# A decoder layer on one core: joint pairs of the FFN prepared one pair ahead, bank-freeing additions put in front, and token sums moved from GpSimd to VectorE

## The chip, the cores and the metric

The kernel runs on one core of a Trainium2 chip. The metric is the device time of one execution in microseconds; several runs are timed and their median is taken. One further execution is profiled. TensorE does the matrix products, VectorE and ScalarE the elementwise work, GpSimd some elementwise work and DMA issues, and SyncE (SP) issues most DMAs.

## What is computed

One layer: RWKV-7 time mixing and indexer-selected sparse attention side by side, merged by gates, then a dense FFN. The change lies in the FFN, d_model 1024, 1024 tokens, FFN width 2816 (22 tiles of 128):

```python
merged = g_a * (y_a @ w_o_rwkv) + g_b * (y_b @ w_o_att)
h = h + merged @ w_out
z = rmsnorm(h, norm2_g) @ w_ffn_in
z_gate, z_up = jnp.split(z, 2, axis=-1)
h = h + (jax.nn.silu(z_gate) * z_up) @ w_ffn_out
return rmsnorm(h, normf_g)
```

## The kernel before

Everything is held with channels on the partitions, in two halves of 512 tokens. A product in float32 precision is made of three float32r matmuls: weights and activations are split into a high and a low part (`split`, L116 the high part on ScalarE, L117 the low part on VectorE), and hi*hi, hi*lo and lo*hi are added up in one PSUM bank (`mm3`, L146, L147, L151). A raw weight tile is loaded into a buffer `wst` (three of them in all), its parts go to `whi` and `wlo` (two of each). Three banks carry the name `acc`, five the name `mix`; a bank is free when VectorE has read it.

The order of TensorE is the order in which the program is written. The other engines are ordered by a scheduler that goes by priority and by its own estimate of time; what stands in `tc.high_priority()` (also called `urgent`) goes ahead. Once built, every engine and every DMA queue works strictly in its order, so an instruction that waits holds up all behind it.

The FFN is done in two ways. The first 8 tiles (`EARLY`) are ordinary: for each half `ffn_in` makes gate and up products of a tile and `ffn_out` adds the product with `w_fo` to h, which lives in DRAM (`d_h`), one output tile d of 8 at a time: load h (L1360), add the bank (L1361), store (L1362). For half 0 this runs as filler work beside RWKV and attention. The filler also holds `ahead(j)`, and half 1's attention loop calls `scaled` eight times: GpSimd adds zhi and zlo, multiplies by the row of norms and stores the normalized half 0 in `d_z`.

Tiles 8 to 21 are *joint*, both halves at once. Halves of the tokens, halves of the input channels and gate/up make a 2x2 by 2x2 block product, done with seven block products instead of eight (Winograd's form of Strassen's scheme). Two of the seven, on half 0 alone, are made by `ahead` and kept in `d_p`. The other five need sums of weight blocks and of token blocks:

- `combined` builds the token blocks t1, t2, t4 from half 1 (`h`) and half 0 (`d_z`, into two tiles `t`), with four GpSimd subtractions for each of four k (L1443), and splits them.
- `joint_in` handles one pair of gate and up tiles j: it loads both weights, makes four GpSimd sums (L1443, scratch tile `s1`, of which there is one), splits them to wb (in whi/wlo), wc (wchi/wclo) and wd (wdhi/wdlo, one buffer each for wc and wd), and then does five products of 12 matmuls: pa, pb, pc, pd, and a second one added into pc's bank (L1495 to L1499). Between them VectorE adds the banks: L1503 (pa), L1505 (pb), L1507 (pc), L1509 (pd), L1512 (pc again). The second product into pc's bank may not begin before L1507 has read it.

After each group of pairs (`JOINT`: 4, 3, 3 and 4 pairs) comes `ffn_out` for both halves, or `finish_out` after the last. A group boundary is the end of `ffn_out` and the start of the next group's first pair. The h tiles of `ffn_out` go through a ring of eight (`more`).

Of the kernel before, what the change touches and what calls it, by code (L numbers as in the profile page):

```python
# [11 lines left out]
F32 = mybir.dt.float32  # L12
# [14 lines left out]
EARLY = [(0, 8)]  # L27
# [23 lines left out]
def block_kernel(ctx: ExitStack, tc: tile.TileContext, ins: dict, outT: bass.AP, stop=None, dbg=None):  # L51
# [1131 lines left out]
    def merge(half, zp, zs, jp=None):  # L1183
# [59 lines left out]
        for d in range(8):  # L1243
# [8 lines left out]
            SY.dma_start(d_h[half][d], h[:, d, :])  # L1252
            sq.add(d, last=half == 1 and d == 7)
# [33 lines left out]
    def ffn_in(half, f, zs, g0, gn):  # L1287

        z, sq = zs[:2]
        for j in range(gn):  # L1290
            pg, pu = acc(), acc()
            src = [ins["w_ffn_in"][2 * (g0 + j) + i] for i in range(2)]
            if g0 + j == 0:
                ws = [weights(x) for x in src]
                first_ = mm3_late([pg, pu], ws, z)
                for i, n in enumerate(first_):
                    yield n
                    if i == 3 and half == 0:
                        sq.columns()
                if half == 0:  # L1300
                    zs.append(sq.row(bufs=2))
                    yield 4
            else:
                yield from mm3(pg, weights(src[0]), z)
                yield from mm3(pu, weights(src[1]), z)
            if half:
                swiglu(f, j, pg, pu)
                continue
            row, x, t = zs[2], tmp(), tmp()
            V.tensor_tensor(x, pg, row, op=ALU.mult)  # L1310
            silu(t, x)
            V.scalar_tensor_tensor(x, pu, 0.5, row, op0=ALU.mult, op1=ALU.mult)
            V.tensor_tensor(t, t, x, op=ALU.mult)
            split(f[0][:, j, :], f[1][:, j, :], t)
# [13 lines left out]
    def ahead(j, zs):  # L1328

        (zhi, zlo), _, row = zs  # L1330
        w = weights(ins["w_ffn_in"][2 * j])
        pss = [acc(), acc()]
        for i, ps in enumerate(pss):
            yield from mm3(ps, w, (zhi, zlo), nk=4, wk=4 * i, ak=4 * i)
# [8 lines left out]
    def scaled(k, zs):  # L1343

        (zhi, zlo), _, row = zs
        x = tmp()
        G.tensor_tensor(x, f32(zhi[:, k, :]), f32(zlo[:, k, :]), op=ALU.add)
        G.tensor_tensor(x, x, row, op=ALU.mult)
        SY.dma_start(d_z[k], x)

    def ffn_out(f, g0, gn, halves, ring=None):

        act = {h: tuple(x[:, gn * i:gn * i + gn, :] for x in f) for i, h in enumerate(halves)}

        def w(d):
            return weights(ins["w_fo"][d][:, g0:g0 + gn, :], gn)

        def add(d, half, ps):
            t = tmp() if ring is None else ring[:, (2 * d + half) % 8, :]
            SY.dma_start(t, d_h[half][d])  # L1360
            V.tensor_tensor(t, t, ps, op=ALU.add)  # L1361
            SY.dma_start(d_h[half][d], t)  # L1362

        first_ = [(d, half) for d in range(2) for half in halves][:2]
        ws = {d: w(d) for d in sorted({d for d, _ in first_})}
        pss = {x: acc() for x in first_}
        yield from mm3_last(list(pss.values()), [ws[d] for d, _ in first_], [act[h] for _, h in first_], gn)
        for d in range(8):
            for half in halves:
                ps = pss.get((d, half))  # L1370
                if ps is None:
                    if d not in ws:
                        ws[d] = w(d)
                    ps = acc()
                    yield from mm3(ps, ws[d], act[half], nk=gn)
                add(d, half, ps)
# [53 lines left out]
    def early(half, zp, zs):  # L1430

        for g0, gn in EARLY:
            f = act_tiles(zp, "f", ("s2", "s0"))
# [280 lines left out]
```

## Time and profile before

| | |
|---|---|
| median of 3 runs | 1774.36 us (1769.57 to 1774.5) |
| profiled execution, its own time | 1764.16 us |
| its span, first to last instruction | 1762.4 us |
| TensorE busy | 1690.7 us, 96% of the span |
| VectorE / ScalarE / GpSimd busy | 1175.9 / 824.5 / 233.5 us |
| mean granted TensorE clock | 0.990 |

Rows of a timeline show the start, the duration, the engine and line, the operation with output and inputs, its shape and, in brackets, how long the engine was idle before and what ended that. In the list of waits each row has the total, the number and the longest. Matmuls are pipelined: one of 512 columns is shown with 0.39 us, though the next begins 0.23 us after it.

### The profile page before, as it was taken

To read this page: it belongs to the slowest core of one execution; us is meant where nothing else is said; L and a number is where in the kernel's file an instruction comes from. 1 tells how busy PE (TensorE), PEld (TensorE's weight loads), DVE (VectorE), ACT (ScalarE), POOL (GpSimd) and SP (SyncE) were. 2 spreads that over 40 slices of the span, in tenths; PEclk is the share of its full clock that TensorE was granted. 3 is DMA by queue.
4 is the path that set the end of the run, shared out by engine and by line. 5 is a ranking of instruction groups with operands and counts; after the bars stand their busy time and mean duration, and the time that the engine had idled before them with its cause. 6 is when DMAs were issued, how large, how long until landed. Compare 5 with 4: busy or idle time off the path is not lost.

```text
span 1762.4 us, 26864 instructions
## 1 busy us (share of the span) xinstructions
PE 1690.7 (96%) x9952; PEld 1386.7 (79%) x9952; DVE 1175.9 (67%) x2253; ACT 824.5 (47%) x1585; POOL 233.5 (13%) x211
## 2 busy tenths in 40 slices
PE   8999999999999999999999899999899999999897
PEld 6888888788877777877887788778688877777787
DVE  5789899866576467857867555665744654655576
ACT  6365998454444787555334367333432221222231
POOL 0000000010022101001000351000600402130420
PEclk9999999999999999999999999999999999999999
DMA  5542224535375425653343883674336436465532
GB/s 208 162 144 95 99 96 142 162 101 178 104 206 158 132 99 177 203 145 117 104 119 124 253 221 121 221 245 149 116 108 195 132 128 215 135 203 163 202 109 96
DMA packets 149091, 268.14 MB, mean 152 GB/s; under 512 B 38704, under 2 KB 63984, under 8 KB 148832
## 3 DMA queue, kind: packets, MB, share of 16 engines
q1 hardware_dynamic: 125600, 192.59, 34.3%
q10 hardware_dynamic: 15552, 47.75, 8.6%
q0 software_dynamic: 7808, 26.09, 5.6%
q8 instruction: 78, 1.28, 0.3%
q14 instruction: 53, 0.43, 0.1%
HBM read 195.54 MB, written 70.83 MB: 151 GB/s over the span
## 4 chain that ended last, share of the span: by engine, by line
PE 67%; DVE 12%; ACT 7%; DMA 6%; issue 4%; POOL 4%; SPq 0%; POOLq 0%; DVEq 0%; ACTq 0%
PE acc L146 14%; PE acc L147 14%; PE acc L151 14%; PE acc L161 3%; PE mix L1495 2%; PE mix L1499 2%; PE mix L1497 2%; DVE wlo L117 2%; PE mix L934 2%; DMA wst<-in_w_ffn_in 2%; PE mix L1093 2%; ACT junk L984 2%; ACT junkl L984 1%; PE mix L1069 1%; POOL wst L1443 1%
## 5 line engine op out<-in xcount | busy, mean ns | idle before, releaser
L117 DVE TENSOR_TENSOR wlo<-wst,whi 128x1024 fp32r<-128x1024 f32 (+2 forms) x201 | 224.2, 1117 | 179.4 <-ACT whi L116 80.4
L116 ACT ACTIVATE whi<-wst 128x1024 fp32r<-128x1024 f32 (+2 forms) x201 | 186.9, 932 | 266.6 <-PE acc L147 194.0
L146 PE MATMUL acc<-zhi,whi 128*128 128x512 f32 x336 | 134.5, 400 | 8.9 <-ACT whi L116 5.6
L146 PE MATMUL acc<-u1hi,whi 128*128 128x512 f32 x352 | 140.7, 400 | 0.1
L147 PE MATMUL acc<-u1lo,whi 128*128 128x512 f32 x352 | 138.4, 393 | 0.0
L146 PE MATMUL acc<-u0hi,whi 128*128 128x512 f32 (+1 forms) x352 | 135.3, 387 | 1.7 <-DVE tmp L352 1.7
L147 PE MATMUL acc<-u0lo,whi 128*128 128x512 f32 (+1 forms) x352 | 133.8, 383 | 0.0
L147 PE MATMUL acc<-zlo,whi 128*128 128x512 f32 x336 | 132.6, 395 | 0.0
L146 PE MATMUL acc<-fhi,whi 128*128 128x512 f32 x236 | 92.9, 394 | 3.2 <-DVE more L1361 2.2
L147 PE MATMUL acc<-flo,whi 128*128 128x512 f32 x236 | 91.9, 389 | 0.0
L151 PE MATMUL acc<-u1hi,wlo 128*128 128x512 f32 x352 | 90.5, 396 | 0.0
L151 PE MATMUL acc<-zhi,wlo 128*128 128x512 f32 x336 | 87.4, 395 | 0.0
L151 PE MATMUL acc<-u0hi,wlo 128*128 128x512 f32 (+1 forms) x352 | 86.6, 385 | 0.0
L146 PEld LDWEIGHTS acc<-zhi,whi 128*128 128x128 f32 x336 | 64.0, 190 | 24.5 <-ACT whi L116 6.7
L146 PEld LDWEIGHTS acc<-u1hi,whi 128*128 128x128 f32 x352 | 67.4, 192 | 14.9 <-DVE tmp L343 0.5
L146 PEld LDWEIGHTS acc<-u0hi,whi 128*128 128x128 f32 x352 | 66.2, 188 | 15.1 <-ACT stg L116 2.1
L147 PEld LDWEIGHTS acc<-u1lo,whi 128*128 128x128 f32 x352 | 67.1, 191 | 13.3
L151 PEld LDWEIGHTS acc<-u1hi,wlo 128*128 128x128 f32 x352 | 65.7, 189 | 14.4 <-issue 1.2
L147 PEld LDWEIGHTS acc<-u0lo,whi 128*128 128x128 f32 x352 | 66.2, 188 | 12.2
L151 PEld LDWEIGHTS acc<-u0hi,wlo 128*128 128x128 f32 x352 | 64.0, 188 | 13.1 <-issue 0.7
L147 PEld LDWEIGHTS acc<-zlo,whi 128*128 128x128 f32 x336 | 64.0, 191 | 12.6
L151 PEld LDWEIGHTS acc<-zhi,wlo 128*128 128x128 f32 x336 | 62.9, 190 | 13.2 <-issue 0.3
(420 smaller groups left out, 3981.2 us busy)
## 6 DMA issues: line engine op xcount, KB each, us to landing
wst<-in_w_ffn_in SPq DMA_DIRECT2D x58, 512.0 KB, 4.0
wst<-in_w_in ACTq DMA_DIRECT2D x36, 512.0 KB, 3.9
wst<-in_w_in SPq DMA_DIRECT2D x27, 512.0 KB, 4.0
k<-d_k POOLq DMA_DIRECT2D x24, 512.0 KB, 8.5
more<-d_h SPq DMA_DIRECT2D x48, 256.0 KB, 3.6
d_h<-more SPq DMA_DIRECT2D x48, 256.0 KB, 3.8
h<-in_xT SPq DMA_DIRECT2D x32, 256.0 KB, 5.0
d_g<-tmp ACTq DMA_DIRECT2D x32, 256.0 KB, 3.0
```

Of the source, the lines that this page charges most:

```text
L116: A.activation(hi, x, AF.Copy)
L117: V.tensor_tensor(lo, x, hi.bitcast(F32), op=ALU.subtract)
L146: T.matmul(ps, whi[:, wk + k, :], ahi[:, ak + k, tok], start=k == 0, stop=False)
L147: T.matmul(ps, whi[:, wk + k, :], alo[:, ak + k, tok], start=False, stop=False)
L151: T.matmul(ps, wlo[:, wk + k, :], ahi[:, ak + k, tok], start=False, stop=k == nk - 1)
L161: T.matmul(ps, w[:, k, :], a[:, k, tok], start=k == 0 and w is whi and a is ahi, stop=k == nk - 1 and a is alo)
L934: T.matmul(ps[:, :w], iq[:, h, :], ik[:, i, c:c + w], start=i == 0, stop=i == 1)
L984: A.activation(junka[:, :n], y, AF.Sign, bias=z[:, i:i + 1], accum_out=cnt[:, i:i + 1])
L1093: T.matmul(py[64 * e:64 * e + 64, bi * 128:(bi + 1) * 128], v[:, j, 64 * e:64 * e + 64], pts[e][j // 4][:, j % 4, :], start=j == b, stop=j ...
L1495: T.matmul(ps, w[0][:, o + k, :], bhi[:, k, :], start=first_ and k == 0, stop=False, skip_group_check=not first_)
L1497: T.matmul(ps, w[0][:, o + k, :], blo[:, k, :], start=False, stop=False, skip_group_check=not first_)
L1499: T.matmul(ps, w[1][:, o + k, :], bhi[:, k, :], start=False, stop=k == 3, skip_group_check=not first_)
```

## The change

1. The weights of a joint pair are handled in two functions. `sums(j)` loads them and makes the four GpSimd sums, `blocks(j)` does the splits. Both are called for pair j+1 at the start of pair j; for the first pair of a group `sums` is called in the last pair of the group before, and `blocks` where `ffn_out` takes its last weight (d = 7). Pair 8 is prepared at d = 7 of half 1's early `ffn_out`.
2. In joint groups the raw output weights go to the two `t` tiles of `combined` instead of `wst`, and half 1 comes before half 0.
3. The additions of pa, pb and pc (now L1527, L1530, L1533) stand in `urgent()`.
4. `scaled` is gone. `merge(0)` stores the raw h in `d_z` as well; `combined` multiplies it by the norm's weight and the row on VectorE when it loads it, and its 16 subtractions are on VectorE too. It takes one of eight steps behind each early tile of half 1.

```diff
             SY.dma_start(d_h[half][d], h[:, d, :])
+            if half == 0:
+                SY.dma_start(d_z[d], h[:, d, :])
...
-    def scaled(k, zs):
-
-        (zhi, zlo), _, row = zs
-        x = tmp()
-        G.tensor_tensor(x, f32(zhi[:, k, :]), f32(zlo[:, k, :]), op=ALU.add)
-        G.tensor_tensor(x, x, row, op=ALU.mult)
-        SY.dma_start(d_z[k], x)
-
-    def ffn_out(f, g0, gn, halves, ring=None):
+    def ffn_out(f, g0, gn, halves, ring=None, raw=None, last=None):
...
         def w(d):
-            return weights(ins["w_fo"][d][:, g0:g0 + gn, :], gn)
+            if d not in ws:
+                src, st = ins["w_fo"][d][:, g0:g0 + gn, :], None
+                if raw is not None:
+                    with tc.high_priority():
+                        st = raw.tile([128, gn, 128], F32, tag="t", name="t", bufs=2)
+                        wq[0].dma_start(st, src)
+                ws[d] = weights(src, gn, st=st)
+                if d == 7 and last is not None:
+                    last()
+            return ws[d]
...
+        def part(ds):
+            for d in ds:
+                for half in reversed(halves):
+                    ps = pss.get((d, half))
+                    if ps is None:
+                        wt, ps = w(d), acc()
+                        yield from mm3(ps, wt, act[half], nk=gn)
+                    add(d, half, ps)
+
+        def open_():
+            for d in range(2):
+                w(d)
+                pss[d, halves[-1]] = acc()
+            yield from mm3_last(list(pss.values()), [ws[0], ws[1]], [act[halves[-1]]] * 2, gn)
+            yield from part(range(2))
...
+        def less(o, a, b):
+            V.tensor_tensor(o, a, b, op=ALU.subtract)
+
         for k in range(4):
...
-            SY.dma_start(a, d_z[k])
-            SY.dma_start(b, d_z[k + 4])
-            pool(ALU.subtract, a, lo, a)
+            for x, i in ((a, k), (b, k + 4)):
+                SY.dma_start(x, d_z[i])
+                V.scalar_tensor_tensor(x, x, par[:, P_N2 + i:P_N2 + i + 1], row, op0=ALU.mult, op1=ALU.mult)
+            less(a, lo, a)
             put(t1, k, a)
-            pool(ALU.subtract, lo, up, lo)
-            pool(ALU.subtract, up, up, a)
+            yield
+            less(lo, up, lo)
+            less(up, up, a)
             put(t2, k, up)
-            pool(ALU.subtract, b, b, up)
+            less(b, b, up)
             put(t4, k, b)
             yield
...
+    prepared = {}
+
+    def sums(j, jp):
+
         with tc.high_priority():
             g, u = (raw_weights(ins["w_ffn_in"][2 * j + e]) for e in range(2))
...
+    def joint_in(f, gn, i, j, bs, ring, jp):
+
+        wb, wc, wd = prepared.pop(j)
+        p1, t0, w, c = (ring[:, j % 2, e, :] for e in range(4))
+        SY.dma_start(ring[:, j % 2, 0:2, :], d_p[j])
+        if j + 1 < NFF:
+            sums(j + 1, jp)
+            if i + 1 < gn:
+                blocks(j + 1, jp)
...
         mm(pa, wb, 0, "t2")
-        V.tensor_tensor(p1, p1, pa, op=ALU.add)
+        with urgent():
+            V.tensor_tensor(p1, p1, pa, op=ALU.add)
...
-                run(ffn_out(f, g0, gn, [0, 1], more))
+                run(*ffn_out(f, g0, gn, [0, 1], more, jp, lambda: blocks(g0 + gn, jp)))
```

TensorE's instructions stand in the same order as before but for the half that comes first in an output tile. What moves is on the other engines. Below, the order of instructions at three places, before and then after.

VectorE at the boundary between the second and the third group, before: wlo, wclo and wdlo are splits of the next pair's weights, s is GpSimd's scratch sum, more the additions that free the output banks, ring the additions of a pair.

```order
L117 TENSOR_TENSOR wlo<-wst,whi 128x384
L1361 TENSOR_TENSOR more<-more,acc 128x512 x2
L117 TENSOR_TENSOR wclo<-wst,wchi 128x1024
L117 TENSOR_TENSOR wdlo<-wst,wdhi 128x512
L117 TENSOR_TENSOR wlo<-wst,whi 128x512
L117 TENSOR_TENSOR wlo<-s_14279,whi 128x512
L1361 TENSOR_TENSOR more<-more,acc 128x512 x3
L117 TENSOR_TENSOR wlo<-s_14381,whi 128x512
L117 TENSOR_TENSOR wlo<-wst,whi 128x512
L1503 TENSOR_TENSOR ring<-ring,acc 128x512
```

The same place after the change, where an output weight comes from t:

```order
L117 TENSOR_TENSOR wlo<-t,whi 128x384
L1362 TENSOR_TENSOR more<-more,acc 128x512 x2
L117 TENSOR_TENSOR wlo<-wst,whi 128x512
L117 TENSOR_TENSOR wlo<-s_13920,whi 128x512
L1362 TENSOR_TENSOR more<-more,acc 128x512 x2
L117 TENSOR_TENSOR wlo<-wst,whi 128x512
L117 TENSOR_TENSOR wlo<-s_14280,whi 128x512
L1362 TENSOR_TENSOR more<-more,acc 128x512
L1527 TENSOR_TENSOR ring<-ring,acc 128x512
```

The wclo and wdlo of the first pair are gone from here (they stand in the last pair of the group before), and one of the three last additions stands behind the second pair's splits.

VectorE in the second pair of the first group, before; the two wlo are the next pair's:

```order
L1512 TENSOR_TENSOR ring<-ring,mix 128x512
L117 TENSOR_TENSOR wlo<-s_13205,whi 128x512
L117 TENSOR_TENSOR wlo<-wst,whi 128x512
L1513 SCALAR_TENSOR_TENSOR ring<-ring 128x512
L1503 TENSOR_TENSOR ring<-ring,acc 128x512
L117 TENSOR_TENSOR flo<-ring,fhi 128x512
L1505 TENSOR_TENSOR ring<-ring,mix 128x512
L1507 TENSOR_TENSOR ring<-ring,mix 128x512
```

And after:

```order
L1538 TENSOR_TENSOR ring<-ring,mix 128x512
L1527 TENSOR_TENSOR ring<-ring,acc 128x512
L117 TENSOR_TENSOR wlo<-wst,whi 128x512
L117 TENSOR_TENSOR wlo<-s_13104,whi 128x512
L1539 SCALAR_TENSOR_TENSOR ring<-ring 128x512
L1530 TENSOR_TENSOR ring<-ring,mix 128x512
L117 TENSOR_TENSOR flo<-ring,fhi 128x512
L1533 TENSOR_TENSOR ring<-ring,mix 128x512
```

The first addition now stands ahead of both splits; the two splits have changed places.

ScalarE at the first early tile of half 1, before; t are high parts of the token blocks, zhi those of half 1, whi a weight:

```order
L1262 ACTIVATE zhi<-h 128x512 x3
L116 ACTIVATE t_12179<-t 128x512
L1262 ACTIVATE zhi<-h 128x512 x2
L1318 ACTIVATE tmp<-tmp 128x512
L116 ACTIVATE t_12180<-h 128x512
L116 ACTIVATE t_12181<-t 128x512
L116 ACTIVATE whi<-wst 128x1024
L1318 ACTIVATE tmp<-acc 128x512
```

And after:

```order
L1264 ACTIVATE zhi<-h 128x512 x5
L1317 ACTIVATE tmp<-tmp 128x512
L116 ACTIVATE whi<-wst 128x1024
L1317 ACTIVATE tmp<-acc 128x512
L116 ACTIVATE t_12139<-t 128x512
L116 ACTIVATE whi<-wst 128x1024
```

The token blocks' copies have moved behind the first weight copy of the second tile.

More of the change, by code (lines that the diff above doesn't have):

```diff
@@ L1285, in mm3_late, with ffn_in @@
             yield 8
[L1287 to L1314, printed above, removed]
+    def ffn_in(half, f, zs, j):
+        z = zs[0]
+        pg, pu = acc(), acc()
+        src = [ins["w_ffn_in"][2 * j + i] for i in range(2)]
+        if j == 0:
+            for i, n in enumerate(mm3_late([pg, pu], [weights(x) for x in src], z)):
+                yield n
+                if i == 3 and half == 0:
+                    zs[1].columns()
+            if half == 0:
+                zs.append(zs[1].row(bufs=2))
+                yield 4
+        else:
+            yield from mm3(pg, weights(src[0]), z)
+            yield from mm3(pu, weights(src[1]), z)
+        if half:
+            swiglu(f, j, pg, pu)
+            return
+        row, x, t = zs[2], tmp(), tmp()
+        V.tensor_tensor(x, pg, row, op=ALU.mult)
+        silu(t, x)
+        V.scalar_tensor_tensor(x, pu, 0.5, row, op0=ALU.mult, op1=ALU.mult)
+        V.tensor_tensor(t, t, x, op=ALU.mult)
+        split(f[0][:, j, :], f[1][:, j, :], t)
     def silu(t, x):
@@ L1333, in ahead @@
         for i, ps in enumerate(pss):
-            yield from mm3(ps, w, (zhi, zlo), nk=4, wk=4 * i, ak=4 * i)
+            yield from mm3(ps, w, zs[0], nk=4, wk=4 * i, ak=4 * i)
+        row = zs[2]
         p, x, t = tmp(), tmp(), tmp()
@@ L1362, in add @@
             SY.dma_start(d_h[half][d], t)
[L1364 to L1376, printed above, removed]
+        def part(ds):
[12 more added lines that the diff above has]
+            yield from part(range(2))
+        return [open_(), *(part([d]) for d in range(2, 8))]
     def norm_out(half, sq):
@@ L1428, in finish_out, with early @@
         run(before)
[L1430 to L1437 removed]
+    def early(half, zp, zs, last=None):
+        f = act_tiles(zp, "f", ("s2", "s0"))
+        return [ffn_in(half, f, zs, j) for j in range(EARLY)], ffn_out(f, 0, EARLY, [half], last=last)
     def f32(x):
@@ L1486, in joint_in, with blocks @@
             pool(ALU.subtract, g2, g2, g1)
-            split(wb[0][:, 0:4], wb[1][:, 0:4], g1)
+        prepared[j] = g, u, s1
+    def blocks(j, jp):
+        g, u, s1 = prepared[j]
+        with tc.high_priority():
+            wb = [wp.tile([128, 8, 128], F32R, tag=t, name=t) for t in ("whi", "wlo")]
+            wc = [jp.tile([128, 8, 128], F32R, tag=t, name=t) for t in ("wchi", "wclo")]
+            wd = [jp.tile([128, 4, 128], F32R, tag=t, name=t) for t in ("wdhi", "wdlo")]
+            split(wb[0][:, 0:4], wb[1][:, 0:4], g[:, 0:4])
             split(wb[0][:, 4:8], wb[1][:, 4:8], s1)
             split(wc[0], wc[1], u)
-            split(wd[0], wd[1], g2)
+            split(wd[0], wd[1], g[:, 4:8])
+        prepared[j] = wb, wc, wd
+    def joint_in(f, gn, i, j, bs, ring, jp):
[6 more added lines that the diff above has]
+                blocks(j + 1, jp)
         def mm(ps, w, o, b, first_=True):
@@ L1617, in block_kernel, with begin @@
         both = [zp0, zp1]
-        build = combined(both, *z1, jp)
-        bs = None
-        for i, n in enumerate(early(1, zp0, z1)):
-            if i % 12 == 11 and i < 48:
-                next(build)
-            if n == 0:
-                bs = next(build)
+        build = combined(both, z0[2], *z1, jp)
+        def begin():
+            sums(JOINT[0][0], jp)
+            blocks(JOINT[0][0], jp)
+        tiles_, outs = early(1, zp0, z1, begin)
+        for i, g in enumerate(tiles_):
+            run(g)
+            next(build)
+        bs = next(build)
+        run(*outs)
         more = jp.tile([128, 8, HT], F32, tag="t3", name="more")
```

36 lines of the change are left out of this document (16 added, 20 removed).

## The prediction

> **What bounds the kernel now.** The page of the profile comes first: TensorE is busy in 96% of the span, so whatever is to be won is the rest of it.
>
> ```profile
> span 1762.4 us, 26864 instructions
> PE 1690.7 (96%) x9952; PEld 1386.7 (79%) x9952; DVE 1175.9 (67%) x2253; ACT 824.5 (47%) x1585; POOL 233.5 (13%) x211
> ```
>
> Next, the busy time by stage (columns: stretch, length, then busy time of TensorE, its weight loads, VectorE, ScalarE, GpSimd). The stretches are the first early tiles of half 1, the other early tiles, and the middle groups of joint pairs.
>
> ```profile
> 1230.00:1282.00 52.00, 44.57 (x182) 34.62 (x181) 42.22 (x50) 23.04 (x35) 31.10 (x16) 0.97 0.37 108
> 1282.00:1378.00 96.00, 95.48 (x422) 78.77 (x421) 39.98 (x48) 28.36 (x35) 6.69 (x5) 1.00 0.52 164
> 1478.00:1563.00 85.00, 79.20 (x342) 64.27 (x343) 49.80 (x73) 18.75 (x30) 19.68 (x14) 0.99 0.55 181
> 1563.00:1644.00 81.00, 75.00 (x322) 60.78 (x321) 44.73 (x66) 17.60 (x28) 16.32 (x12) 0.98 0.53 173
> ```
>
> The second row is the floor: 422 matmuls in 95.48 us, 0.226 us each. The first loses 7.4 us, the last two about 6 us each. The waits of TensorE from 1230 to 1712 us say to whom (total, times, longest):
>
> ```profile
> PE acc L1495 <- DVE more L1361: 8.6, 2, 4.4
> PE mix L1495 <- DVE ring L1507: 6.7, 6, 1.5
> PE acc L146 <- ACT whi L116: 6.1, 3, 3.5
> PE acc L146 <- DVE more L1361: 2.2, 1, 2.2
> PE acc L1280 <- ACT zhi L1262: 1.7, 2, 1.0
> ```
>
> Together 25.3 us, and the change touches the first four kinds. The timeline of TensorE gives their places, and a second cost: how it restarts.
>
> ```profile
> 1253.04 0.50 PE L146 MATMUL acc<-zhi,whi 128*128 128x512 f32 x1 [3.46 <-ACT whi L116]
> ...
> 1254.54 0.61 PE L146 MATMUL acc<-zhi,whi 128*128 128x512 f32 x1
> ...
> 1257.93 0.41 PE L146 MATMUL acc<-zhi,whi 128*128 128x512 f32 x1
> ...
> 1278.97 0.50 PE L146 MATMUL acc<-zhi,whi 128*128 128x512 f32 x1 [2.14 <-ACT whi L116]
> ...
> 1403.48 0.50 PE L1495 MATMUL mix<-t,wchi 128*128 128x512 f32 x1 [0.96 <-DVE ring L1507]
> ...
> 1478.22 0.50 PE L146 MATMUL acc<-fhi,whi 128*128 128x512 f32 x1 [2.21 <-DVE more L1361]
> ...
> 1561.14 0.47 PE L1495 MATMUL acc<-t,whi 128*128 128x512 f32 x1 [4.22 <-DVE more L1361]
> ...
> 1643.35 0.50 PE L1495 MATMUL acc<-t,whi 128*128 128x512 f32 x1 [4.38 <-DVE more L1361]
> ```
>
> Soon after the 3.46 us stall eight matmuls, from 1254.54 to 1257.93, take 3.39 us instead of 8 x 0.226 = 1.81: a restart costs 1.6 us. I charge it to the three stalls of 3.4 us and more and not to those near 2 us.
>
> **Group boundaries (after the output tiles of a group).** The chain of waits shows why the 4.22 us arise; the last row is VectorE's timeline.
>
> ```profile
> 1545.37 6.07 DMA wst<-in_w_ffn_in
> ...
> 1552.94 1.29 POOL wst L1443
> ...
> 1555.68 2.14 POOL wst L1443
> ...
> 1557.84 0.64 ACT wdhi L116
> ```
> ```profile
> 1560.32 1.88 DVE L1361 TENSOR_TENSOR more<-more,acc 128x512 f32<-128x512 f32 x3
> ```
>
> The next pair's up-weight is loaded only from 1545.37, because its buffer was held by output weights. GpSimd's sums follow, then the splits, and the three bank-freeing additions stand behind those splits on VectorE, though their banks were full long before. After the change the four sums of that pair are issued during the last pair of the group, before its eight output weights, which have their own two buffers. What is left at the boundary is the split of two 128x512 blocks. It needs the whi/wlo buffer of output tile 6, free when TensorE has left that tile; tile 7 then covers 18 matmuls x 0.226 = 4.1 us in a group of three and 24 x 0.226 = 5.4 us in a group of four. Two ScalarE copies at about 0.6 us and two VectorE splits at about 0.6 us fit in. So all three stalls should go: 2.21 + 4.22 + 4.38 = 10.8 us, and two restarts, 3.2 us: **14.0 us**.
>
> What is late next? In the new order VectorE takes the splits of the second pair's first blocks ahead of the last addition of the group. These wait for GpSimd's sums of the second pair, whose one scratch tile (s1) is free only after the first pair's split: about 1.8 us into tile 7, then three additions of 1.3 to 2.1 us (rows 1552.94 and 1555.68), so 4 to 6 us more, then 1.2 us of splits. That is 3 to 5 us into the first pair. What must not be late there is the addition that frees its third bank, due 48 matmuls, 10.9 us, in; covered. The wclo split of the next group now stands in the last pair, waits there for the last matmuls of that pair, and has the flo of half 1, the last ring addition and half 0's flo queued behind it. TensorE needs half 1's flo about 14 matmuls after the pair's end (groups of three), 3.2 us, and it is ready after that split, 2 x 0.6 us, and its own 0.7; the half 0 one can be late by half a microsecond, as much as now. Bounds: 14.0 down to 9 if a residue of 1.6 us stays at each place.
>
> **Token sums behind early tiles.** Rows of ScalarE's timeline, then of GpSimd's, then of VectorE's:
>
> ```profile
> 1250.07 0.63 ACT L116 ACTIVATE t<-h 128x512 fp32r<-128x512 f32 x1 [7.24 <-POOL h L1443]
> ...
> 1251.95 1.04 ACT L116 ACTIVATE whi<-wst 128x1024 fp32r<-128x1024 f32 x1
> ```
> ```profile
> 1241.82 6.86 POOL L1443 TENSOR_TENSOR h<-h 128x512 f32<-128x512 f32 x1 [7.77 <-DVE zlo L1265]
> ```
> ```profile
> 1243.84 3.09 DVE L1265 TENSOR_TENSOR zlo<-h,zhi 128x512 fp32r<-128x512 f32 x5
> ```
>
> ScalarE's weight copy stood behind two token copies, and these behind a GpSimd subtraction of 6.86 us. The 2.14 us at 1278.97 is the same thing one step later. Now the weight copy stands before all token copies (the third quoted order), and the 16 subtractions and 8 scalings run on VectorE at 3.09 / 5 = 0.6 us: 24 x 0.6 = 14.4 us more, mostly over eight early tiles, where it is busy 39.98 of 96 us in the later ones. Each tile gives it 48 matmuls, 10.9 us, and asks, at 0.6 us for 128x512, 4.2 us of its own (two weight splits of double size, two gate steps, one split) and 2.7 us of token work (one scaling, two subtractions, one and a half splits), so nothing is late. The token loads share SP's queue with weight loads that are needed some 10 us after their issue. Gain 3.46 + 2.14 + one restart 1.6 = **7.2 us**; at worst the second stall stays: 5.
>
> **Bank-freeing additions.** The third addition of a pair (L1507, L1533 after) should be done while TensorE works on the fourth product. Rows of VectorE around the 0.96 us stall, and GpSimd's sum that it waits for:
>
> ```profile
> 1398.82 1.22 DVE L117 TENSOR_TENSOR wlo<-wst,whi 128x512 fp32r<-128x512 f32 x1 [1.84 <-ACT whi L116]
> ...
> 1402.74 0.69 DVE L1507 TENSOR_TENSOR ring<-ring,mix 128x512 f32<-128x512 f32 x1
> ```
> ```profile
> 1396.50 1.62 POOL L1443 TENSOR_TENSOR wst<-s,wst 128x512 f32<-128x512 f32 x1
> ```
>
> VectorE waits at this wlo for sums that begin when the up-weight has landed. That load waits for one of three wst buffers, which the change doesn't add to. Behind the wait stood five instructions up to and with L1507; in the new order the first addition (L1503) has moved ahead of the wait, but the second wlo has moved behind it, and five are left again. So I give back only 0.3 us at each of six places for a shorter wait for fhi and less traffic beside GpSimd: **2.0 us**, between 0 and 6.7. The Trainium skill (Perfetto Trace Analysis, Optimization Strategy) reads a gap that repeats on the saturated engine as a sign of too few buffers for the next tile; by that the six gaps stay whole and the sum below is 21.5 instead of 23.5. The six waits of 6.7 us agree with it so far.
>
> **Scaling of half 0 taken off GpSimd.** Eight pairs of operations leave the attention of half 1. One of them disturbed VectorE and then TensorE (rows of GpSimd, VectorE, TensorE):
>
> ```profile
> 1001.33 1.29 POOL L1347 TENSOR_TENSOR tmp<-zhi,zlo 128x512 f32<-128x512 f32 x1 [17.42 <-DVE mx L1071]
> ```
> ```profile
> 1001.38 1.79 DVE L1319 SCALAR_TENSOR_TENSOR tmp<-tmp 128x512 f32<-128x512 f32 x1 [0.33 <-ACT tmp L1318]
> ```
> ```profile
> 1004.64 0.77 PE L1083 MATMUL mix<-kc,L 128*128 128x128 f32 x5 [1.62 <-ACT L L1074]
> ```
>
> 1.79 - 0.69 = **1.1 us** of the 1.62 goes; 0 to 1.6. In exchange eight d_z stores of raw h follow the d_h stores on SP, much earlier; each is one issue of about 0.3 us and comes once per output tile, so nothing: 0 to 2 us.
>
> **A wait that is added.** In the merge of half 1 VectorE now scales the first token tile ahead of a weight split and of the addition that ends a stall there (TensorE, VectorE, SP):
>
> ```profile
> 1133.86 0.47 PE L146 MATMUL acc<-yhi,whi 128*128 128x512 f32 x1 [2.40 <-DVE mid L1199]
> ...
> 1135.49 0.63 PE L146 MATMUL acc<-yhi,whi 128*128 128x512 f32 x1
> ```
> ```profile
> 1133.03 0.69 DVE L1199 SCALAR_TENSOR_TENSOR mid<-tmp,acc 128x512 f32<-128x512 f32 x1 [0.78 <-DMA tmp<-d_g]
> ```
> ```profile
> 1127.49 0.32 SPq L1456 DMA_DIRECT2D t<-d_z  x1
> ```
>
> The scaling waits for that load; behind it are the wlo of the next output weight and mid, which frees the bank. The load is issued 5.5 us before mid, so I take one instruction and a little: **-0.8 us**, 0 to -3.
>
> **The sum.** 14.0 + 7.2 + 2.0 + 1.1 - 0.8 = 23.5 us. From the profiled execution, 1764.16 us, that is 1740.7; its 1764.16 lies 10.2 us under the median of the runs, 1774.36, and they are what will be compared: 1774.36 - 23.5 = 1750.9 us. All bounds on the good side give 14.0 + 7.2 + 6.7 + 1.6 = 29.5 us, and a run-to-run spread of some 5 us stands in the three times; on the bad side 9 + 5 + 0 + 0 - 3 - 2 = 9 us.
>
> **The rivals.** *The boundary wait comes back* (chance 0.15). VectorE's in-order line decides: if the second pair's up-weight gets its buffer only after the first pair's split, lands 6.07 us later and is summed behind that, the splits end some 9 us into the pair, and the additions behind them start a new stall at each boundary, 2.4 to 4 us with a restart. Of 14.0 us some 4 are left, the total gain is near 12 us: 1762. For it: these splits stand before two additions in the new order. Against: 10.9 us of cover. The Trainium skill (TensorE: Matmul & The Clock Gate, What's actually happening) lets the clock fall only after an idle window of about 3.4 us, so that such a stall would cost its length alone; the trace disagrees, since the row at 1135.49, soon after the 2.40 us stall, has the slow 0.63 us too.
>
> *Nothing that can be measured* (0.08). About 0.3%, 5.3 us, is what a measurement of this kernel can tell from no change. It needs both the boundary and the early gain to fall to a third; the time is 1771.
>
> *Slower: SP's queue becomes the bound of the output tiles* (0.06). The landing times on the page:
>
> ```profile
> more<-d_h SPq DMA_DIRECT2D x48, 256.0 KB, 3.6
> d_h<-more SPq DMA_DIRECT2D x48, 256.0 KB, 3.8
> ```
>
> The load of an output weight is now tied to two t buffers and stands between loads and stores of h in one in-order queue. If per output tile SP waits once for a store's landing (3.8 us) and issues five transfers at 0.33 us, it needs 5.4 us; that decides as soon as it exceeds the tile's 4.1 us in a group of three, and with two such waits, 9.2 us, it loses 5.1 us in six tiles of two groups and 3.8 us in six of one: 84 us, less 23.5, some 1835 us. Against: a weight is asked for two tiles ahead of its split, and the ring of eight h tiles lets stores land long before.
>
> **How the numbers follow.** The forecast, a gain of 15 us or more, has 0.71. The likeliest time is 1751. The range runs from 1740, the good bounds with the runs' spread, to 1767, which holds the returning boundary wait; the last two rivals are left out. Faster by over 0.3%: 0.71 + 0.15 = 0.86; same 0.08; slower 0.06.
>
> **What would show it.** Right: no TensorE wait on the additions of output tiles (L1362 after) at the three boundaries, none of over 0.5 us on whi after the first and third early tile, no GpSimd work among the early tiles, and six waits of 0.5 to 1.3 us on L1533 still there. Wrong: a new wait on the first pair of a group, waits for wlo<-t or for w_fo loads among output tiles, a merge stall over 3 us, or the six pair waits gone.

## The result and the profile after

| | before | after |
|---|---|---|
| median | 1771.96 us (4 runs, 1765.48 to 1774.5) | 1742.66 us (4 runs, 1741.6 to 1744.95) |
| profiled execution, its own time | 1764.16 us | 1742.06 us |
| its span | 1762.4 us | 1740.3 us |
| mean granted TensorE clock | 0.990 | 0.992 |

The ratio is 0.9842, with an interval of 0.9811 to 0.9873. The kernel became faster by 22.1 us between the two profiled executions and by 29.3 us between the medians. First the page of the profile after:

```profile
span 1740.3 us, 26809 instructions
PE 1681.8 (97%) x9952; PEld 1382.1 (79%) x9952; DVE 1178.5 (68%) x2277; ACT 823.6 (47%) x1585; POOL 177.2 (10%) x179
```

TensorE does the same 9952 matmuls, and GpSimd has lost 56 us. The busy times by stage, in stretches laid at the same places as the four of before (columns as there; GpSimd is the fifth time). The three that lost time before now hold 8 to 19 matmuls more:

```profile
1226.00:1270.00 44.00, 42.99 (x190) 34.70 (x189) 41.64 (x60) 21.95 (x32) 0.00 (x0) 1.00 0.44 141
1270.00:1366.00 96.00, 95.48 (x421) 78.75 (x420) 46.77 (x58) 29.50 (x37) 5.79 (x4) 1.00 0.51 165
1463.00:1546.00 83.00, 81.81 (x360) 67.07 (x360) 48.27 (x70) 19.16 (x31) 20.96 (x15) 1.00 0.60 190
1546.00:1625.00 79.00, 77.47 (x341) 63.52 (x340) 47.78 (x70) 19.15 (x31) 17.68 (x13) 1.00 0.58 184
```

The first early tiles lose 1.0 us instead of 7.4, and the groups of pairs 1.2 and 1.5 us instead of 5.8 and 6.0. VectorE is at 41.64 of 44 us in the first stretch, and TensorE doesn't wait for it. The waits of TensorE from 900 to 1760 us:

```profile
PE acc L146 <- DVE tmp L1335: 7.4, 1, 7.4
PE mix L1518 <- DVE ring L1533: 7.2, 6, 2.7
PE acc L146 <- DVE mid L1199: 2.7, 1, 2.7
...
PE acc L146 <- ACT whi L116: 1.0, 2, 0.5
...
PE acc L147 <- DVE flo L117: 1.0, 2, 0.5
```

The rows on L1361 (8.6 + 2.2 us) have no successor, and whi is down from 6.6 us in the same stretch to 1.0. The six pair waits are all there, 7.2 us instead of 6.7. One row is new at the head of the list: 7.4 us on the first addition of an `ahead` product, near 995 us; it was 2.9 us before. Where the 22 us came from, by the starts of the same matmuls in both profiles, so with restarts:

| place | us |
|---|---|
| three group boundaries | -14.9 |
| early tiles, whi | -7.9 |
| early tiles, zhi | -1.1 |
| half 1's attention (near 1004 and 1022 us) | -2.1 |
| merge of half 1 | -1.3 |
| six pair waits | +0.5 |
| flo and fhi after the pairs of the last three groups | +1.1 |
| stall near 995 us | +5.4 |
| before 960 us, which the change doesn't touch | -2.6 |
| rest | +0.8 |

### The profile page after: what moved, and what is told of

Same layout as the page of the kernel before. It is cut to its first block, busy times and chain, and to the rows that moved or that the text cites. A ratio compares the mean times of both kernels' runs of the same rounds, so it can differ in the third digit from the quotient of the medians.

```text
span 1740.3 us, 26809 instructions
## 1 busy us (share of the span) xinstructions
PE 1681.8 (97%) x9952; PEld 1382.1 (79%) x9952; DVE 1178.5 (68%) x2277; ACT 823.6 (47%) x1585; POOL 177.2 (10%) x179
## 4 chain that ended last, share of the span: by engine, by line
PE 61%; DVE 9%; DMA 4%; ACT 3%; issue 2%; POOL 2%; SPq 0%; POOLq 0%; DVEq 0%; ACTq 0%
PE acc L146 14%; PE acc L151 13%; PE acc L147 13%; DVE wlo L117 2%; PE mix L1093 2%; PE mix L1518 2%; PE acc L161 2%; PE mix L1069 2%; PE mix L1522 2%; PE mix L1520 2%; PE mix L1083 2%; DMA wst<-in_w_ffn_in 1%; DMA d_h<-tmp 1%; PE mix L828 1%; PE mix L840 1%
## 5 line engine op out<-in xcount | busy, mean ns | idle before, releaser
L117 DVE TENSOR_TENSOR wlo<-wst,whi 128x1024 fp32r<-128x1024 f32 (+1 forms) x177 | 210.1, 1189 | 159.2 <-ACT whi L116 89.6
L116 ACT ACTIVATE whi<-wst 128x1024 fp32r<-128x1024 f32 (+1 forms) x177 | 173.9, 984 | 221.3 <-PE acc L147 147.9
L151 PEld LDWEIGHTS acc<-u1hi,wlo 128*128 128x128 f32 x352 | 65.7, 189 | 14.4 <-issue 1.2
```

The source lines that it names most:

```text
L116: A.activation(hi, x, AF.Copy)
L117: V.tensor_tensor(lo, x, hi.bitcast(F32), op=ALU.subtract)
L151: T.matmul(ps, wlo[:, wk + k, :], ahi[:, ak + k, tok], start=False, stop=k == nk - 1)
```

## The experiments

Nine other kernels were run, and before and after once more: the first four beside each other on one chip, so the next four, and the last three. Before had medians of 1769.4, 1771.8 and 1769.2 us there. All kernels here compute the whole layer.

**Additions no longer in front.**

```diff
-        with urgent():
-            V.tensor_tensor(p1, p1, pa, op=ALU.add)
+        V.tensor_tensor(p1, p1, pa, op=ALU.add)
...
```

> The three additions of a pair are taken out of urgent(); all else is the changed kernel (1742.7 us). Theory: the boundary gain of 14 us comes from the next pair's sums being a group's eight output tiles ahead, so the boundary stalls stay away and the six waits on the third addition stay near the 7.2 us of the changed kernel: 1741 to 1746 us. Rival: the additions in front free the banks and bring the boundary gain: the three stalls of 2 to 4.4 us return, 1754 to 1758 us.

Measured: 1746.4 us (1743.3 to 1748.4), ratio 0.9869 (0.9846 to 0.9891). The waits of this kernel, and a stall in its third group:

```profile
PE mix L1518 <- DVE ring L1530: 9.6, 5, 3.0
```
```profile
1571.04 0.80 PE L1518 MATMUL mix<-t,wchi 128*128 128x512 f32 x1 [2.50 <-DVE ring L1530]
1571.63 0.63 PE L1520 MATMUL mix<-t,wchi 128*128 128x512 f32 x1
```

No boundary stall came back: the rival falls. But the pair waits grew from 7.2 to 9.6 us, and three of them brought slow restarts (the 0.63 us row), so the additions in front are worth 2.4 us of waits, and 6.9 us of lost time from 1380 to 1700 us in the two profiles. The medians differ by 2 to 4 us (1742.7 and 1744.5 for the changed kernel), which lies within the spread of its executions (1739.8 to 1749.2 us). They hold down a wait that the other parts had raised from 6.7.

**Output weights through wst again.**

```diff
-                run(*ffn_out(f, g0, gn, [0, 1], more, jp, lambda: blocks(g0 + gn, jp)))
+                run(*ffn_out(f, g0, gn, [0, 1], more, None, lambda: blocks(g0 + gn, jp)))
```

> Sums stay one pair ahead, but the raw output weights go through wst again. Theory: the raw pair of the next group holds two of the three wst buffers during the whole stretch of output tiles, so output weights go through one buffer, load after split: some 5 to 6 us for a tile of 4.1 us (groups of three) or 5.4 us (four), waits of TensorE on whi among output tiles of 10 to 35 us in all, 1752 to 1778 us. Rival: sums ahead alone bring the gain and the own buffers do nothing: 1741 to 1746 us.

Measured: 1744.4 us (1739.0 to 1748.9), ratio 0.9857 (0.983 to 0.9885). No wait among output tiles, no boundary stall. My theory falls here: the own buffers are not needed. Its premise was wrong, because wclo and wdlo are split in the last pair of the group before, so that the raw up-weight gives its wst back before the output tiles begin, and two are left for them.

**Sums called late, own buffers kept.**

```diff
-        if j + 1 < NFF:
+        if i + 1 < gn:
             sums(j + 1, jp)
-            if i + 1 < gn:
-                blocks(j + 1, jp)
+            blocks(j + 1, jp)
...
-                run(*ffn_out(f, g0, gn, [0, 1], more, jp, lambda: blocks(g0 + gn, jp)))
+                run(*ffn_out(f, g0, gn, [0, 1], more, jp, lambda: (sums(g0 + gn, jp), blocks(g0 + gn, jp))))
```

> The output weights keep their own buffers, but the sums for the first pair of a group are issued only where the group before takes its last output weight (d = 7), as its splits are. Theory: load, four GpSimd sums of 1.3 to 2.1 us and two splits need some 12 us behind that point, more than the two tiles left, 8 to 11 us, so stalls of 1 to 4 us with restarts return at the three boundaries: 1747 to 1757 us. Rival: own buffers alone bring the gain, because the loads no longer wait for an output weight's buffer: 1741 to 1745 us.

Measured: 1745.1 us (1743.2 to 1748.3), ratio 0.9869 (0.9845 to 0.9893), no boundary stall. It was no test of late sums: with buffers free, the scheduler put the loads and sums as early as in the changed kernel. The second pair's first sum of the third group starts at 1540.76 us after 35.88 us of idle GpSimd, in the changed kernel at 1541.95 us after 35.83: in both, the first pair's sums were done 35 us before.

**Both ways closed**: sums called at d = 7, and output weights through wst (the two edits above together).

> Both ways to early sums are closed: the sums for the first pair of a group are called at d = 7, and the raw output weights go through wst, so that the up-weight's load stands behind output weights' buffers. The token part, the order of halves and the additions in front stay as changed. Theory: the boundary gain comes from early sums and either way alone suffices, so here wclo and wdlo stand again before the last additions of the output tiles and wait for late sums: three stalls of 2 to 4.4 us with restarts return, 14 us more than the changed kernel, 1752 to 1758 us. Rival: the gain comes from the order of halves or of the splits at d = 7, which stay: 1742 to 1746 us.

Measured: 1763.6 us (10 runs, 1759.9 to 1767.9), ratio 0.996 (0.994 to 0.998): 21 us more than the changed kernel where 14 were expected. The waits of TensorE, and VectorE at the second boundary:

```profile
PE acc L1517 <- DVE more L1362: 11.6, 2, 6.4
PE acc L146 <- DVE more L1362: 5.6, 1, 5.6
PE mix L1517 <- DVE ring L1532: 5.1, 6, 1.8
```
```profile
1553.79 1.33 DVE L117 TENSOR_TENSOR wclo<-wst,wchi 128x1024 fp32r<-128x1024 f32 x1 [4.81 <-ACT wchi L116]
...
1558.75 1.88 DVE L1362 TENSOR_TENSOR more<-more,acc 128x512 f32<-128x512 f32 x3
```

This settles the boundary. The three stalls are back, 17.2 us and longer than before (10.8), and VectorE has the same picture as before: three bank-freeing additions behind a wclo that waits for late sums. The order of halves, the splits at d = 7 and the additions in front were all still there. So early sums are what brings the boundary gain, and either the early call or the own buffers is enough to get them.

**Token sums back on GpSimd**, with pairs and output tiles as changed.

```diff
-        def less(o, a, b):
-            V.tensor_tensor(o, a, b, op=ALU.subtract)
...
-            less(a, lo, a)
+            pool(ALU.subtract, a, lo, a)
...
+            if i % 8 == 4 and i < 64:
+                scaled(i // 8, z0)
```

> The token sums are put back on GpSimd (subtractions L1443 of before, the eight scalings in half 1's attention, d_z normalized), in the first four early tiles as before; pairs and output tiles stay as changed. Theory: the stalls on whi behind the first and third early tile (3.5 and 2.1 us with a restart of 1.6) and the zhi and attention waits return: 8 to 11 us more than the changed kernel, 1750 to 1754 us. Rival: those stalls came from the order of the early tiles' weights, which stays changed: 1742 to 1745 us.

Measured: 1755.0 us (1750.6 to 1756.9), ratio 0.9915 (0.9891 to 0.9939), 10.5 to 12.3 us more than the changed kernel. TensorE and ScalarE of this kernel among the early tiles:

```profile
1254.33 0.50 PE L146 MATMUL acc<-zhi,whi 128*128 128x512 f32 x1 [0.81 <-ACT whi L116]
...
1280.33 0.50 PE L146 MATMUL acc<-zhi,whi 128*128 128x512 f32 x1 [2.19 <-ACT whi L116]
```
```profile
1251.33 0.63 ACT L116 ACTIVATE t<-h 128x512 fp32r<-128x512 f32 x1 [7.26 <-POOL h L1450]
...
1253.24 1.04 ACT L116 ACTIVATE whi<-wst 128x1024 fp32r<-128x1024 f32 x1
```

The stalls are back (5.4 us on whi in all), with the cause that the prediction named: a weight copy behind token copies that wait for GpSimd. The subtractions and the scalings went back together, so which of the two does what is told by the places alone. The waits in the attention (1.87 us near 1005 us, 1.67 us near 1024 us) are back too, and the stall near 995 us is 3.2 us here instead of 7.4, which a later part takes up.

**Splits behind the third addition.** The next pair's wlo splits are written, and kept, behind L1533.

```diff
         if j + 1 < NFF:
             sums(j + 1, jp)
-            if i + 1 < gn:
-                blocks(j + 1, jp)
...
-            V.tensor_tensor(c, w, pc, op=ALU.add)
+            tc.keep_in_program_order(V.tensor_tensor(c, w, pc, op=ALU.add))
+        if j + 1 < NFF and i + 1 < gn:
+            blocks(j + 1, jp)
...
+                tc.keep_in_program_order(
+                    V.tensor_tensor(wb[1][:, o:o + 4], x, wb[0][:, o:o + 4].bitcast(F32), op=ALU.subtract))
```

> The splits of the next pair's wb stand behind the addition of pc on VectorE (fixed order); buffers and sums are unchanged. Theory: the six pair waits (7.2 us) arise because the third addition stands behind a split that waits for late sums; with the order turned they go, and the late split has the 24 matmuls (5.4 us) after that addition as cover: 7 to 10 us less than the changed kernel, 1733 to 1737 us, if the first pair of a group doesn't wait for its next weights in place of it. Rival: the lateness of the sums sets the time whatever the order, and the wait moves to the first product of the next pair (TensorE on wlo or whi): 1741 to 1745 us.

Measured: 1733.8 us (1732.0 to 1738.2), ratio 0.9798 (0.9773 to 0.9823). None of the six pair waits is left, and nothing takes their place. GpSimd, VectorE and TensorE of the changed kernel at the longest of them, then VectorE at the same place of this one:

```profile
1640.82 1.29 POOL L1444 TENSOR_TENSOR wst<-s,wst 128x512 f32<-128x512 f32 x1
```
```profile
1642.80 1.23 DVE L117 TENSOR_TENSOR wlo<-wst,whi 128x512 fp32r<-128x512 f32 x1 [5.37 <-ACT whi L116]
...
1646.54 0.68 DVE L1533 TENSOR_TENSOR ring<-ring,mix 128x512 f32<-128x512 f32 x1
```
```profile
1647.27 0.50 PE L1518 MATMUL mix<-t,wchi 128*128 128x512 f32 x1 [2.69 <-DVE ring L1533]
```
```profile
1640.65 0.69 DVE L1533 TENSOR_TENSOR ring<-ring,mix 128x512 f32<-128x512 f32 x1
1641.26 0.68 DVE L1502 TENSOR_TENSOR wlo<-wst,whi 128x512 fp32r<-128x512 f32 x1
1641.86 0.69 DVE L1502 TENSOR_TENSOR wlo<-s,whi 128x512 fp32r<-128x512 f32 x1
```

Above, the engine stands 5.37 us at a split that nobody needs yet, with five instructions behind it, the bank-freeing one last. The sum is there at 1642.1 and the bank is due at 1644.6 (1647.27 less the 2.69 of waiting), but from the split to the addition six instructions are worked off first. Below, the addition goes ahead and the splits follow. At this place the sum also comes 1.8 us earlier by the pair's own time, but that alone isn't what took the waits away: in the six pairs of this kernel the sum that VectorE stands at ends 3.4 to 4.1 us before the bank is due, and in the changed kernel five pairs whose sum ends 3.7 to 4.6 us before still wait 0.4 to 1.7 us.

**Every second up-weight in buffers of its own.**

```diff
-            g, u = (raw_weights(ins["w_ffn_in"][2 * j + e]) for e in range(2))
+            g = raw_weights(ins["w_ffn_in"][2 * j])
+            if own:
+                u1, u2 = (jp.tile([128, 4, 128], F32, tag="t", name="t", bufs=2) for _ in range(2))
+                for i, x in enumerate((u1, u2)):
+                    SY.dma_start(x, ins["w_ffn_in"][2 * j + 1][:, 4 * i:4 * i + 4, :])
...
-            sums(j + 1, jp)
+            sums(j + 1, jp, i % 2 == 0 and i + 1 < gn)
```

> Every second raw up-weight of a group goes in two halves to the two t tiles instead of wst, so a pair's raw weights have room two pairs ahead; the order on VectorE stays. Theory: the sums are late because the up-weight's load waits for one of three wst buffers; with room the load starts earlier, the splits no longer wait, and the pair waits fall from 7.2 us to under 3: 1735 to 1740 us. Rival: the loads are held by something else (their place on the queue, GpSimd's in-order sums behind s1): 1741 to 1745 us, with the six waits still there.

Measured: 1752.9 us (1747.5 to 1759.7), ratio 0.9892 (0.9862 to 0.9922): slower than the changed kernel by 8 to 10 us. The theory falls; the waits are there, as its rival had it, but longer. The profiled execution was the slowest of the four. The waits, then VectorE, SP and GpSimd at the second pair of the last group:

```profile
PE mix L1526 <- DVE ring L1541: 13.5, 6, 4.1
```
```profile
1646.97 1.29 DVE L117 TENSOR_TENSOR wclo<-t,wchi 128x512 fp32r<-128x512 f32 x2
...
1659.84 1.20 DVE L117 TENSOR_TENSOR wlo<-wst,whi 128x512 fp32r<-128x512 f32 x1 [1.82 <-ACT whi L116]
1660.96 0.67 DVE L1541 TENSOR_TENSOR ring<-ring,mix 128x512 f32<-128x512 f32 x1
```
```profile
1647.68 0.93 SPq L1487 DMA_DIRECT2D t<-in_w_ffn_in  x2
```
```profile
1654.82 1.28 POOL L1444 TENSOR_TENSOR s<-t 128x512 f32<-128x512 f32 x1 [8.58 <-DMA t<-in_w_ffn_in]
```

A raw up-weight keeps its buffer until the wclo split, which can only be made when the pair before has used the one wchi. So the next use of t can't load before 1647.68, its sums start at 1654.82, and the bank-freeing addition stands behind the splits that need them. More room made the wait longer, 4.1 us here instead of 2.7. This is one form of more room, which brings a wait of its own; three whole buffers more weren't tried.

**Loads of the attention held.** GpSimd's loads of the next head pair's v and q wait, as k's do, for the present pair's sums.

```diff
+            if behind is not None:
+                for h in range(half + 1):
+                    G.tensor_copy(v[:, 4 * h, 0:2], behind)
...
+            if behind is not None:
+                G.tensor_copy(q[:, 0, 0:2], behind)
```

> In half 1's attention GpSimd's loads of the next head pair's v and q are held, as those of k are, until the present head pair's sums exist (small GpSimd copies that write into the tiles first). Theory: before the change the scaling on GpSimd stood in front of these loads and held them back; without it some 0.8 MB more flow beside the stores of the last early output tiles, whose landing of up to 18 us holds up VectorE and then TensorE for 7.4 us near 995 us of the span (2.9 us before the change). Held, the stall falls to 3 us or less: 2 to 5 us less than the changed kernel, 1738 to 1741 us. Rival: the stores land late for another reason, since the stall varied from 4.4 to 7.4 us between kernels that are alike there: 1741 to 1745 us.

Measured: 1748.1 us (1742.2 to 1749.1), ratio 0.9868 (0.9842 to 0.9894): no gain, and over both expected ranges. The stall near 995 us fell to 2.0 us, 6.2 us won against the changed kernel by the starts of the matmuls, but 30 us later TensorE waited 3.3 us for q, 5.1 us with its restart. A transfer that came too early now came too late. A slow restart in the merge took another 2.9 us; why it came isn't known.

**Splits behind the addition, and loads held for a shorter time** (until the present pair's first maxima, `mx`, some 3 us before).

```diff
+                    G.tensor_copy(v[:, 4 * h, 0:2], mxs[hp - 1])
...
+            if half and hp:
+                G.tensor_copy(q[:, 0, 0:2], mxs[hp - 1])
```

> The kernel with the splits behind the third addition (1733.8 us), and in half 1's attention GpSimd's loads of the next head pair's v and q held until the first maxima of the present head pair exist, some 3 us earlier than in the kernel that held them for the sums. Theory: the stall near 995 us falls from 4.4 to 7.4 us to about 2, and q arrives in time: 2 to 5 us less, 1729 to 1732 us. Rival: the wait for q at the second head pair comes back as it did before (3.3 us) and eats the gain: 1732 to 1736 us.

Measured: 1730.1 us (1729.5 to 1731.2), ratio 0.9793 (0.9778 to 0.9807). This beats both kernels: 39.1 us under before and 14.4 us under the changed one on the same chip. Its span is 12.6 us under that of the changed kernel's first profile: 8.9 us less at the pair waits, 5.3 us less at the stall near 995 us and the attention behind it, 1.9 us more in the merge. No wait for q came back. The times don't show the second part apart: against before, the kernel with the splits alone had 0.9798, this one 0.9793. VectorE at this stall, and the stores and GpSimd's queue (q0) from 955 to 1003 us, in before, after and this kernel:

```profile
993.02 0.69 DVE L1336 TENSOR_TENSOR tmp<-acc,row 128x512 f32<-128x512 f32 x1 [7.83 <-DMA d_h<-tmp]
```
```profile
q0 software_dynamic: 1008, 3.41, 26.6%
...
d_h<-tmp SPq DMA_DIRECT2D x4, 256.0 KB, 8.8
```
```profile
995.00 0.69 DVE L1335 TENSOR_TENSOR tmp<-acc,row 128x512 f32<-128x512 f32 x1 [12.34 <-DMA d_h<-tmp]
```
```profile
q0 software_dynamic: 1280, 4.20, 31.9%
...
d_h<-tmp SPq DMA_DIRECT2D x4, 256.0 KB, 18.2
```
```profile
989.70 0.69 DVE L1341 TENSOR_TENSOR tmp<-acc,row 128x512 f32<-128x512 f32 x1 [7.08 <-DMA d_h<-tmp]
```
```profile
q0 software_dynamic: 960, 3.27, 26.6%
...
d_h<-tmp SPq DMA_DIRECT2D x4, 256.0 KB, 12.9
```

0.8 MB more on GpSimd's queue, and VectorE waits 12.3 instead of 7.8 us for a store; with the loads held, 7.1, though the median store there takes 12.9 us. In the eight profiles with these loads free the stall of TensorE was 4.2 to 7.4 us, in the five with them held, or with the scaling ahead of them on GpSimd, 2.0 to 3.2 us.

**Before and after once more**, unchanged.

> The kernel before, unchanged, with another profile, since its median lies 10 us over its profiled execution. Theory: the added time of its slower executions lies in the waits on transfers and restarts that the change takes away or shifts (the boundaries, the early tiles, the stall near 995 us), each 1 to 3 us longer: 1766 to 1774 us. Rival: it is spread evenly, by a lower granted clock: the same waits, and more time in every stretch.

> The changed kernel, unchanged, beside the two others on one chip. Its time was 1741.6 to 1745.0 us, so 1740 to 1747 us. The stall near 995 us, 4.4 to 7.4 us in six kernels that are alike there, should lie in that range, and the six pair waits near 7 us.

Measured: before 1771.1 us (1765.7 to 1773.5), after 1744.5 us (1739.8 to 1749.2; ratio 0.9865, 0.9843 to 0.9887). The waits of the second profile of before, whose span is 1770.2 us, and one wait in its attention:

```profile
PE acc L1495 <- DVE more L1361: 10.8, 2, 6.3
```
```profile
1022.48 0.53 PE L1069 MATMUL mix<-k,q 128*128 128x320 f32 x2 [1.96 <-POOL tmp L1347]
```

Its 7.8 us over the first profile lie at two kinds of places: 5.1 us at the three boundaries (the last stall is 6.3 instead of 4.4 us, with longer restarts) and 2.6 us in the attention near 1022 us, where TensorE now waits for the scaling on GpSimd. The other differences are under 1.6 us each and cancel. Both kinds of waits are things that the change removes. The stall near 995 us and the waits on whi, which the theory also named, were shorter than in the first profile. In after's second profile the stall near 995 us is 4.2 us, just under what was expected, the pair waits 5.9 us; most of its 6.5 us over the first lie between 600 and 800 us, which the change doesn't touch.

## Why the prediction was right, and where it was wrong

The forecast (1751 us, a gain of 15 us or more) came true in its kind; the time lies 8 us under it, near the good end of the range. Of what was to show it right, the six pair waits are there, but with 0.4 to 2.7 us instead of 0.5 to 1.3.

*Boundaries, 14.0 us:* measured 14.9. The cause, late sums in front of bank-freeing additions, is shown by undoing it. The eight own buffers' part in it was wrong: the own buffers weren't needed. What was to be late next, the second pair's splits, ended 4.1 us into the first pair (its first matmul is at 1544.39), within the 3 to 5 predicted, and cost nothing:

```profile
1546.68 1.23 DVE L117 TENSOR_TENSOR wlo<-wst,whi 128x512 fp32r<-128x512 f32 x1 [3.45 <-ACT whi L116]
1547.83 0.68 DVE L117 TENSOR_TENSOR wlo<-s,whi 128x512 fp32r<-128x512 f32 x1
1548.43 0.68 DVE L1362 TENSOR_TENSOR more<-more,acc 128x512 f32<-128x512 f32 x1
```

The half microsecond on half 0's flo came, 0.48 us in each group of three; "as much as now" was misread, since before has no such wait there.

*Token sums, 7.2 us:* measured 7.9, and 1.1 more on zhi, which I hadn't counted. ScalarE after, at the place of the 3.46 us stall, has the weight copies between the token copies and waits for none of them:

```profile
1246.42 1.06 ACT L116 ACTIVATE whi<-wst 128x1024 fp32r<-128x1024 f32 x1 [5.01 <-PE acc L1286]
...
1247.86 0.62 ACT L116 ACTIVATE t<-t 128x512 fp32r<-128x512 f32 x1
1248.38 1.05 ACT L116 ACTIVATE whi<-wst 128x1024 fp32r<-128x1024 f32 x1
```

*Bank-freeing additions, 2.0 us:* failed; the waits went from 6.7 to 7.2. By place, the step "back only 0.3 us at each of six places" came out at four: 0.96, 1.24, 1.51 and 0.79 us became 0.43, 0.71, 1.05 and 0.63. The second wait grew from 1.22 to 1.70 us, and the fifth, in the second pair of the last group, from 0.96 to 2.69. The step took the lateness of the sums as given, and at these two the sums come later. At the fifth the sum that VectorE stands at ends 2.3 us before the bank is due, where it was 4.2. GpSimd there, after the change:

```profile
1627.46 4.31 POOL L1400 DMA_DIRECT2D h<-d_h  x8 [4.54 <-issue]
1638.09 1.28 POOL L1444 TENSOR_TENSOR s<-wst 128x512 f32<-128x512 f32 x1 [6.33 <-DMA wst<-in_w_ffn_in]
```

The sums' weight loads are issued 12.6 and 8.8 us before the bank is due, in before as in after. But GpSimd's eight loads of h for the last output tiles (2.1 MB) now end their issue 12.7 us before that time, right ahead of the weights, and not 16.7 us. In the seven profiles with early sums and the old order on VectorE (the kernel with an up-weight in other buffers left out) these loads end 9.3 to 12.7 us before, and the wait is 2.2 to 3.0 us; in the two of before and in the kernel with sums late again they end 16.7 to 17.8 us before, and it is 0.7 to 1.0 us. Nearly all of the difference between the 5.1 us of pair waits in that kernel and the 7.2 us lies at this place. That the loads of h hold up the weights is read from this, and wasn't tested. The additions in front work against it: without them the changed kernel has 9.6 us.

I had also put the root in the three wst buffers. What can be cured is the place of the wait in VectorE's order: turning that took all six waits away, with sums that at five of the six places came no earlier, and more room in the form tried did not. The Trainium skill (Perfetto Trace Analysis, Optimization Strategy) says that a gap which repeats on the engine that should be saturated can mean too little room for the next tile; from that I had the six gaps stay, and they did. But as a reading of these gaps it fits badly: with more room 13.5 us, with another order none.

*Scaling off GpSimd, 1.1 us:* measured 2.1 in the profiled pair, since a second wait near 1022 us went as well, and 4.6 us against the second profile of before, in which that wait is on the scaling itself.

*The wait added in the merge, -0.8 us:* the wait is there, as named, and the stall grew from 2.40 to 2.74 us, but no slow restart followed it, so the place gained 1.3 us. I had charged no restart to stalls near 2 us, though the row at 1135.49 showed one here; why it stayed away after the change isn't known, so this gain is luck. VectorE after:

```profile
1133.03 0.75 DVE L1462 SCALAR_TENSOR_TENSOR t<-t,par,row 128x512 f32<-128x512 f32 x1 [1.96 <-DMA t<-d_z]
...
1134.30 0.68 DVE L1199 SCALAR_TENSOR_TENSOR mid<-tmp,acc 128x512 f32<-128x512 f32 x1
```

*Not foreseen, -5.4 us:* the scaling stood in front of GpSimd's loads and held them back. GpSimd before, behind the scaling at 1001.33, and after:

```profile
1002.56 0.76 POOL L1047 DMA_DIRECT2D v<-d_v  x1
```
```profile
983.68 0.75 POOL L1047 DMA_DIRECT2D v<-d_v  x1 [2.55 <-DMA k<-d_k]
```

I had costed what leaves GpSimd by who waits for it, and not by what stands behind it on its queue.

*The sum and the base.* The terms add up to 23.5 us, against 22.1 in the profiled pair. That they lie so near is in part luck: the pair waits, the stall near 995 us and flo cost 9 us that weren't in the sum, and some 8 us came in that weren't either, 2.6 of them before 960 us, which the change doesn't touch, and 2.1 at the merge. The 8 us by which the time was missed lie in the step from one execution to the median. 2.4 us of them are the median of before, 1771.96 us and not 1774.36 with one run more. The others are the difference of 29.3 and 23.5 us: I took the sum from the median of before as if its executions differed elsewhere. In its second profile, of an execution at the median (1772.0 us), they differ at the boundaries and at the scaling, 5.1 + 2.6 us, so the median execution had more to lose than the profiled one. This rests on one profile. On one chip the gain was 24.7 us (1769.2 to 1744.5), and the changed kernel's own executions lie up to 9 us apart there.

*A rival's price.* For "nothing that can be measured" I had both gains fall to a third. By my own terms that leaves 7.1 + 2.0 + 1.1 - 0.8 = 9.4 us, which would have been measured; they would have had to fall further.

## What to carry to other kernels

Ask of each wait of an in-order engine what stands behind it: a split that nobody needed yet cost 2.7 us because the instruction that frees a bank stood behind it, and a change of order cured what more room, in the one form tried, made worse. When work on an engine that also issues transfers is taken off or moved, look at what it had been holding back, and time those transfers on purpose. And when the median lies over the profiled execution, find where the other executions are slower before a gain is taken from the median: here, by one more profile, it was at the very places that the change touches.

## What the chip showed that I had not expected

- The length of a stall doesn't decide alone whether TensorE restarts slowly. After 2.50 us (1571 us, without the additions in front) and 2.40 us (before, merge) matmuls came every 0.43 us for a while; after 2.74 us (after, merge) and 2.69 us (after, 1647 us) they came every 0.23 us almost at once. Over all thirteen profiles, among 512-column matmuls from 980 us on, the shortest stall with a slow restart was 1.84 us (both ways closed, 1410 us) and the longest without one 3.09 us (output weights through wst, 1138 us); all of 3.2 us and more had one. What decides between the two stays open here. The Trainium skill (TensorE: Matmul & The Clock Gate, What's actually happening) has the clock fall after an idle window of about 3.4 us; the slow restarts after 1.84, 2.40 and 2.50 us disagree, if a window is to be idle throughout.
- From 955 to 1003 us stores of 256 KB landed after a median of 15.0 to 18.2 us in the eight profiles with 4.2 MB on GpSimd's queue beside them, and after 8.5 to 9.1 us in the three with 3.4 MB. With the loads held, beside 3.2 and 3.3 MB, it was 12.8 and 12.9 us, so the bytes on that queue alone don't decide.
